# Seven block products in place of eight in 20 of 22 blocks of an FFN's up product, and a down product in three groups

## The chip, the cores and the metric

The kernel runs on one core of a Trainium2 chip. The metric is the device time of one launch in microseconds (us). Before the change three runs took 1074.0, 1075.09 and 1076.6 us; 1075.09 us is the median. The profile is of one further execution on the chip. Engines are named PE (matrix products), PEld (its weight loads), ACT (ScalarE), DVE (VectorE), POOL (GpSimd) and SP (which issues most transfers).

## The reference

One layer of a decoder step for 512 prompt tokens and 8 sequences of 4 new tokens, 544 columns in all. Two mixers (gated linear attention and dilated window attention) come first; the change is in the FFN at the end:

```python
x = x + g1 * (merged @ w_out)
h2 = _rmsnorm(x, norm2_g) * (1 + sc2) + sh2
u1, u2 = jnp.split(h2 @ w_up, 2, axis=-1)
x = x + g2 * ((jax.nn.silu(u1) * u2) @ w_down)
```

With `D_MODEL` 1024 and `D_FF` 2816, `w_up` is 1024 x 5632 and `w_down` 2816 x 1024. A last norm gives the output `y`. Everything is float32.

## The kernel before

Activations lie feature-major: a tile is 128 features by T = 544 columns (NH = 272 is a half). A float32 product is made from three float32r products: each operand is split into a rounded part `hi` and a rest `lo` (ACT casts, DVE subtracts), and PE adds `hi*hi`, `hi*lo` and `lo*hi` in PSUM.

`fm_tile` (L480) makes one 128-row output tile: for every block of 128 inputs six matmuls (`mm_k`, L474, L476, L478), three for each half of the columns. The two halves go to the two banks of one PSUM tile `mm`, of which there are two; a second pool, `sd`, has four one-bank tiles. Weights stream in pieces of 1 MB through three `raw` buffers (L409); `w_split` splits chunks of 128x1024 ahead of their use (ACT L421, DVE L422) into two `hi` and two `lo` buffers.

The order of each engine's work is the order in which the program issues it (`manual_schedule`); waits between engines are put in by the tile layer. In `ffn` (L1694):

- Three up tiles are made by column halves, while the modulated input `h2` is still being finished (L1718 to L1720). Then 41 up tiles follow by `fm_tile`, 8 inputs each, in the order u1, u2 of block 0, of block 1 and so on. `up_evac` takes Silu of u1 (ACT L1688), multiplies by u2 (DVE L1690) and splits the result (ACT L495, DVE L496).
- Seven down tiles follow, 22 inputs each; `residual` (DVE L1546 to L1554) adds them to `x`.
- The last down tile is made half by half (`half_tile`, L1610 to L1612), so that the output of the first half (`out`, L1757) is computed beside the second half's matmuls.

`mid` (L1614) makes the tiles ahead of the FFN; its two last tiles go half by half too (`last_two`, L1596).

Of the kernel before, what the change touches and what calls it, by code (L numbers as in the profile page):

```python
# [6 lines left out]
F32 = mybir.dt.float32  # L7
F32R = mybir.dt.float32r
AF = mybir.ActivationFunctionType
# [4 lines left out]
D = 1024  # L14
NP = 512
# [34 lines left out]

def up_order():
    seq = []
    for m in range(KF):
        seq += [("u1", m), ("u2", m)]
    return seq
# [15 lines left out]
def prep(inp):  # L71
# [32 lines left out]
    wu = inp["w_up"][0]  # L104
    uo = [wu[:, (0 if n == "u1" else DFF) + 128 * m:(0 if n == "u1" else DFF) + 128 * (m + 1)] for n, m in up_order()]
    u3 = slab(np.concatenate(uo[:3], 1))
    sl += wos[:6] + [u3[:, :1024]] + wos[6:] + [u3[:, 1024:]] + [slab(u) for u in uo[3:]]
    wd = inp["w_down"][0]
    sl += [slab(wd[:, 128 * m:128 * (m + 1)]) for m in range(7)]
    wl = np.zeros((128, 24 * 128), f)  # L110
    wl[:, :KF * 128] = slab(wd[:, 896:])
    A["wlast"] = np.ascontiguousarray(wl.reshape(128, 6, 512).transpose(1, 0, 2))
    cols = np.concatenate(sl, 1)
# [204 lines left out]
class Body:  # L318
# [78 lines left out]
    def w_init(self):  # L397
        self.raw = {}
        self.chunks = {}
        self.npiece = 0  # L400
        self.nchunk = 0
        self.pos = 0
        self.total = self.I["wst"].shape[0]

# [8 lines left out]
    def w_split(self, upto):  # L413
        while self.nchunk <= min(upto, 2 * self.total - 1):
            c = self.nchunk
            p = c // 2
            self.w_dma(p + 1)
# [167 lines left out]
    def run(self):  # L585
        nc, tc, I, O = self.nc, self.tc, self.I, self.O
        with ExitStack() as es:
            P = lambda **k: es.enter_context(tc.tile_pool(**k))
            self.cp = P(name="const", bufs=1)
            self.sm = P(name="small", bufs=2)  # L590
            self.heap = P(name="heap", bufs=59)
            self.rawp = P(name="rawp", bufs=3)
            self.hip = P(name="hip", bufs=2)
# [10 lines left out]
            self.heap2 = P(name="heap2", bufs=14)  # L604
            self.ffn()

# [1038 lines left out]
    def h2_half(self, k, half):  # L1645
# [13 lines left out]
        if half == 1:  # L1659
# [7 lines left out]
            nc.gpsimd.tensor_copy(hi[:, NP:T], self.xs[:, k, :])  # L1667
            nc.gpsimd.tensor_sub(lo[:, NP:T], self.xs[:, k, :], hi[:, NP:T])

        def rest():  # L1670
# [9 lines left out]
    def up_evac(self, n, m, halves, hs=(0, 1)):  # L1680
# [10 lines left out]
        if n == "u2" and hs[-1] == 1:  # L1691
            self.act[m] = self.split(self.su.pop(m), "act", self.heap2 if m < 7 else None)

    def ffn(self):  # L1694
# [3 lines left out]
        self.su = {}  # L1698
        uo = up_order()
        ps3 = [[t] for t in self.halves(self.mm()) + [self.mm()[:, 0, :NH]]]  # L1700
        ws = self.ws3
        for half in range(2):
# [3 lines left out]
            if half == 1:  # L1706
                for i in range(3):
                    self.up_evac(*uo[i], ps3[i], (0,))
                    ps3[i].append(self.sd()[:, :NH])
                self.w_split(self.pos // 8 + 1)  # L1710
            c0, c1 = self.COLS[half]
            seq = [(k, m) for k in range(KD) for m in range(3)]
            seq = [(0, 0), (0, 1), (1, 0), (1, 1), (0, 2), (1, 2)] + seq[6:]
            for k, m in seq:
# [6 lines left out]
                if (half, k, m) == (0, 2, 0):  # L1721
                    self.last_rstd(1)
        h2 = self.h2
        self.h2 = self.xa = self.ws3 = None
        self.rst = self.ssq = self.sqh = ws = None
        L0.append(self.copy_rest())
        for i in range(3):
            self.up_evac(*uo[i], ps3[i], (1,))
        for i in range(3, 2 * KF):
            ps = self.fm_tile(h2)  # L1730
            self.up_evac(*uo[i], self.halves(ps))
            self.pump()
        h2 = None
        act = self.act
        ws = []
        L1.append(self.last_weights(ws))
        for m in range(7):
            ps = self.fm_tile(act)
            for h in range(2):
                self.residual(ps[:, h, :NH], self.G2, m, h)  # L1740
            self.sumsq_add(m)
            nc.scalar.mul(self.x[m], self.x[m], self.c("nfg")[:, m:m + 1])
            if m == 6:
                self.act_set(6)
            self.pump()
        while any(self.lanes) or self.late:
            self.pump()

        def out(half):
            c0, c1 = self.COLS[half]  # L1750
            x7 = self.x[7][:, c0:c1]
            nc.scalar.mul(x7, x7, self.c("nfg")[:, 7:8])
            for j in range(4):
# [7 lines left out]

        pss = [self.mm()[:, 0, :NH] for _ in range(2)]
        self.sqh = {}
        for half in range(2):
            ps = pss[half]
# [7 lines left out]
            if half == 0:  # L1773
                self.sqh[7] = self.t2("sq")
            nc.scalar.activation(self.sqh[7][:, c0:c1], self.x[7][:, c0:c1], AF.Square)
        self.last_rstd(1, self.sqh[7])
        out(1)

    def last_weights(self, ws):

        prev = None
        for i in range(7):
            nxt = None
            if i < 6:
# [37 lines left out]
```

## Time and profile before

| what | value |
|---|---|
| median of three runs | 1075.09 us |
| the profiled execution | 1073.69 us |
| its span, first to last instruction | 1071.9 us |
| mean granted PE clock | 0.994 |
| PE busy, matmuls | 1054.3 us (98%), 8505 |
| DVE busy | 447.3 us (42%) |
| ACT busy | 374.9 us (35%) |
| POOL busy | 154.2 us (14%) |

Busy shares are means over stages. A PE matmul row has the time from its start to its modelled end, and matmuls overlap: the distance between starts is the pace. A time such as 652.59 is microseconds from the start of the span. The FFN's plain up tiles run from 679.64 to the end of the up product, the down tiles after them to about 1060.3.

### The profile page before, as it was taken

What the parts mean: (1) busy time and instruction counts of PE and PEld (TensorE: products, weight loads), DVE (VectorE), ACT (ScalarE), POOL (GpSimd) and SP (SyncE); (2) the same over time, 40 slices, a digit from 0 to 9 for tenths busy, and PEclk for the clock granted to TensorE, in tenths of its full rate; (3) what the DMA queues carried; (4) which work ended last, traced back from release to release, by engine and by line L of the source; (5) the groups of instructions that cost most, each with busy time, mean ns of one, the idle gap of its engine ahead of it and who ended that gap; (6) DMA issues with size and microseconds to landing.
All of it is one profiled execution on the core that took longest, in us unless ns stands there. A gap on an engine that the chain in (4) does not pass through costs nothing.

```text
span 1071.9 us, 19534 instructions
## 1 busy us (share of the span) xinstructions
PE 1054.3 (98%) x8505; PEld 988.1 (92%) x8505; DVE 447.3 (42%) x696; ACT 374.9 (35%) x600; POOL 154.2 (14%) x203
## 2 busy tenths in 40 slices
PE   9999999999999999999999999999999999999996
PEld 8788679999989999998989999999999999999995
DVE  5562333444442476353225767433233333332333
ACT  5561214444426432541143335422222323232322
POOL 2302003442332000110011431100000000000101
PEclk9999999999999999899999999999999999999998
DMA  9746563441124427725886563265322222332202
GB/s 375 306 147 237 182 241 127 144 164 65 64 79 162 155 83 239 276 99 150 290 304 207 192 221 153 104 251 235 138 79 106 91 79 79 108 119 90 98 1 84
DMA packets 48701, 169.60 MB, mean 158 GB/s; under 512 B 4124, under 2 KB 27004, under 8 KB 33260
## 3 DMA queue, kind: packets, MB, share of 16 engines
q1 hardware_dynamic: 47928, 167.43, 43.3%
q8 instruction: 67, 1.10, 0.4%
q10 hardware_dynamic: 688, 0.93, 0.3%
q14 instruction: 18, 0.15, 0.0%
HBM read 144.29 MB, written 36.63 MB: 169 GB/s over the span
## 4 chain that ended last, share of the span: by engine, by line
PE 89%; DVE 3%; issue 3%; ACT 2%; POOL 1%; DMA 1%; SPq 0%; DVEq 0%; ACTq 0%; POOLq 0%
PE mm L474 22%; PE mm L478 22%; PE mm L476 22%; PE mm L978 2%; PE mm L980 2%; PE mm L979 2%; PE sd L512 2%; PE sd L1348 1%; POOL o L1390 1%; PE sd L841 1%; PE sd L957 1%; PE sd L825 1%; PE sd L1175 1%; PE sd L1180 1%; POOL sq L1383 1%
## 5 line engine op out<-in xcount | busy, mean ns | idle before, releaser
L422 DVE TENSOR_TENSOR lo<-raw,hi 128x1024 fp32r<-128x1024 f32 x132 | 164.1, 1244 | 191.1 <-ACT hi L421 190.7
L421 ACT CAST hi<-raw 128x1024 fp32r<-128x1024 f32 x132 | 138.3, 1049 | 96.7 <-PE mm L476 91.8
L474 PE MATMUL mm<-hh,hi 128*128 128x272 f32 x656 | 139.2, 293 | 1.3 <-ACT lr L728 1.0
L474 PE MATMUL mm<-h2h,hi 128*128 128x272 f32 x656 | 136.0, 288 | 0.0
L476 PE MATMUL mm<-hl,hi 128*128 128x272 f32 x656 | 135.8, 288 | 0.0
L478 PE MATMUL mm<-hh,lo 128*128 128x272 f32 x656 | 135.7, 288 | 0.1
L476 PE MATMUL mm<-h2l,hi 128*128 128x272 f32 x656 | 135.4, 288 | 0.0
L478 PE MATMUL mm<-h2h,lo 128*128 128x272 f32 x656 | 135.3, 287 | 0.0
L474 PEld LDWEIGHTS mm<-hh,hi 128*128 128x128 f32 x656 | 102.5, 188 | 9.4 <-issue 4.0
L478 PEld LDWEIGHTS mm<-hh,lo 128*128 128x128 f32 x656 | 103.0, 188 | 0.3 <-DVE lo L422 0.3
L476 PEld LDWEIGHTS mm<-h2l,hi 128*128 128x128 f32 x656 | 103.1, 188 | 0.0
L476 PEld LDWEIGHTS mm<-hl,hi 128*128 128x128 f32 x656 | 102.8, 188 | 0.0
L474 PEld LDWEIGHTS mm<-h2h,hi 128*128 128x128 f32 x656 | 102.7, 188 | 0.0
L478 PEld LDWEIGHTS mm<-h2h,lo 128*128 128x128 f32 x656 | 102.7, 188 | 0.0
L1563 POOL TENSOR_TENSOR sq<-sq,sq 128x544 f32<-128x544 f32 x11 | 15.0, 1364 | 365.8 <-ACT sq L1559 365.8
L474 PE MATMUL mm<-acth,hi 128*128 128x272 f32 x308 | 63.8, 288 | 0.0
L476 PE MATMUL mm<-actl,hi 128*128 128x272 f32 x308 | 63.7, 288 | 0.0
L478 PE MATMUL mm<-acth,lo 128*128 128x272 f32 x308 | 63.7, 288 | 0.0
L1051 ACT ACTIVATE qs<-mm,ca 32x544 f32<-32x544 f32 x48 | 33.9, 707 | 56.4 <-PE mm L478 51.2
L495 ACT CAST acth<-su 128x544 fp32r<-128x544 f32 x22 | 14.3, 649 | 110.8 <-DVE su L1690 110.8
L978 PE MATMUL mm<-hi,hh 128*128 128x512 f32 (+1 forms) x128 | 49.0, 383 | 0.0
L478 PEld LDWEIGHTS mm<-acth,lo 128*128 128x128 f32 x308 | 48.3, 188 | 0.0
(354 smaller groups left out, 1832.9 us busy)
## 6 DMA issues: line engine op xcount, KB each, us to landing
raw<-in_wst_dram SPq DMA_DIRECT2D x69, 1024.0 KB, 4.8
ada<-in_wada_dram SPq DMA_DIRECT2D x24, 1024.0 KB, 7.2
out_rest_dram<-in_rest_dram SPq DMA_DIRECT2D x16, 768.0 KB, 7.0
out_kn_dram<-kg SPq DMA_DIRECT2D x5, 1024.0 KB, 6.0
x<-in_xT_dram SPq DMA_DIRECT2D x16, 272.0 KB, 5.2
kg<-in_kg_dram SPq DMA_DIRECT2D x4, 1032.0 KB, 9.4
s<-in_s_dram SPq DMA_DIRECT2D x4, 1024.0 KB, 5.0
vg<-in_vg_dram SPq DMA_DIRECT2D x4, 1024.0 KB, 5.9
```

Source lines behind the costliest of these rows:

```text
L421: self.nc.scalar.copy(hi, src)
L422: self.nc.vector.tensor_sub(lo, src, hi)
L474: nc.tensor.matmul(outs[h], lhsT=wh, rhs=xh[:, h * NH:(h + 1) * NH], start=first, stop=False)
L476: nc.tensor.matmul(outs[h], lhsT=wh, rhs=xl[:, h * NH:(h + 1) * NH], start=False, stop=False)
L478: nc.tensor.matmul(outs[h], lhsT=wl, rhs=xh[:, h * NH:(h + 1) * NH], start=False, stop=last)
L495: self.nc.scalar.copy(hi, src)
L512: nc.tensor.matmul(pa[32 * j:32 * j + 32, :256], lhsT=c[:, 32 * k:32 * k + 32], rhs=w[:, 256 * k:256 * k + 256], start=(k < 4), stop=(k >= 4))
L978: nc.tensor.matmul(out(tt), lhsT=xh, rhs=wh, start=(k == 0), stop=False)
L979: nc.tensor.matmul(out(tt), lhsT=xh, rhs=wl, start=False, stop=False)
L980: nc.tensor.matmul(out(tt), lhsT=xl, rhs=wh, start=False, stop=(k == KD - 1))
L1051: nc.scalar.activation(self.two(qs)[32 * q:32 * q + 32], ps[32 * s:32 * s + 32, :, :NH], AF.Identity, bias=b[32 * s:32 * s + 32])
L1563: nc.gpsimd.tensor_add(self.ssq, self.ssq, s)
```

## The change

For the blocks 2 to 21 the pair of up tiles (u1, u2) is seen as a 2 x 2 product: the inputs in two halves (features 0 to 511 and 512 to 1023), the columns in two halves, and the outputs u1 and u2. Strassen's scheme (in Winograd's form) makes it from seven products of half the input depth, M1 to M7, in place of eight. A product is 4 input blocks x 3 matmuls = 12 matmuls of 272 columns; a block takes 84 matmuls in place of 96. The sums that it needs:

- of inputs, once: `combos` makes eight tiles `ta`, `tb` (POOL L1725, DVE L1726 to L1730) and splits them;
- of weights, per block: `s_sums` (four POOL instructions of 128x512); the seven weight operands are split by `s_a`, `s_b`, `s_c` (128x1024 each) and `s_d` (128x512);
- of outputs, per block: M1+M2, and the sums over M5, M6, M3, M7, M4, which PE accumulates in the two banks `a` and `c` of one `mm` tile, with copies of partial sums by ACT (L1811, L1829, L1832) and sums by DVE (L1824, L1838, L1841).

The down product is made in groups of 8, 8 and 6 blocks, each for all eight output tiles, and added to `x` by `residual`; so the residual step runs 24 times in place of 8. The last group ends with two tiles half by half (`down_last`). `hip` has three buffers in place of two, `heap` 62 in place of 59.

```diff
+GROUPS = [range(0, 8), range(8, 16), range(16, KF)]
...
+    def s_mm(self, n, i, out, first=True, last=True):
+        wh, wl = self.W[n].pop(i)
+        for k in range(4):
+            w = slice(128 * k, 128 * k + 128)
+            xh, xl = self.s_in(i, k)
+            for j, (a, b) in enumerate(((wh, xh), (wh, xl), (wl, xh))):
+                nc.tensor.matmul(out, lhsT=a[:, w], rhs=b, start=first and k == 0 and j == 0,
+                                 stop=last and k == 3 and j == 2, skip_group_check=True)
...
+    def s_first(self, n):
+        ps = self.mm()
+        a = ps[:, 0, :NH]
+        self.s_mm(n, 1, a)
+        t = self.t2("sA")
+        self.nc.scalar.copy(t[:, :NH], a)
+        self.open[n] = (a, ps[:, 1, :NH], t)
+
+    def s_run(self, run, after):
+        nc = self.nc
+        for n, nxt in zip(run, run[1:] + [None]):
+            if nxt:
+                self.s_sums(nxt)
+            a, c, t = self.open.pop(n)
+            su, u, s5 = self.t2("su"), self.t2("u"), self.t2("s5")
+            b = self.sd()[:, :NH]
+            self.s_mm(n, 2, b)
+            nc.vector.tensor_add(su[:, :NH], b, t[:, :NH])
+            nc.scalar.activation(su[:, :NH], su[:, :NH], AF.Silu)
+            if nxt:
+                self.s_a(nxt)
+            self.s_mm(n, 5, c)
+            nc.scalar.copy(s5[:, :NH], c)
+            self.s_d(n)
+            self.s_mm(n, 6, a, False)
+            nc.scalar.copy(t[:, NH:], a)
+            if nxt:
+                self.s_b(nxt)
+            else:
+                after()
+            self.s_mm(n, 3, c, False)
+            nc.vector.tensor_add(su[:, NH:], c, t[:, NH:])
+            nc.scalar.activation(su[:, NH:], su[:, NH:], AF.Silu)
+            self.s_mm(n, 7, a, False)
+            nc.vector.tensor_add(u[:, NH:], a, s5[:, :NH])
+            nc.vector.tensor_mul(u[:, NH:], u[:, NH:], su[:, NH:])
+            if nxt:
+                self.s_c(nxt)
+                self.s_first(nxt)
+            self.s_mm(n, 4, a, False)
+            nc.vector.tensor_mul(u[:, :NH], a, su[:, :NH])
+            self.act[n] = self.split(u, "act")
...
     def ffn(self):
...
+        self.s_sums(2)
+        self.TC = []
+        for q in range(4):
+            self.TC.append(self.combos(q))
+            if q == 1:
+                for i in range(3):
+                    self.up_evac(*UP0[i], ps3[i], (1,))
+        self.s_a(2)
+        ps = self.fm_tile(self.h2)
+        self.up_evac(*UP0[3], self.halves(ps))
+        self.s_b(2)
+        self.s_first(2)
+        self.s_c(2)
...
-        for m in range(7):
+        for m in range(6):
...
-            self.half_tile(ps, act, ws, half, 0, 12)
-            if half == 1:
-                self.last_rstd(0, self.sqh[7])
-                out(0)
-            self.half_tile(ps, act, ws, half, 12, KF)
-            self.residual(ps, self.G2, 7, half)
+            for m in (6, 7):
+                o = ps[m][:, half, :NH]
+                self.half_tile(o, act, ws[n * (m - 6):n * (m - 5)], half)
+                if (half, m) == (1, 6):
+                    self.last_rstd(0, sq[1])
+                    out(0)
+                self.residual(o, self.G2, m, half)
```

On PE, an up tile of before, where rows of all 8 inputs follow each other; `[waits ...]` names the engine whose count an instruction waits for:

```order
L474 MATMUL mm_7817<-h2h_6717,hi_7761 128x272 x2
L476 MATMUL mm_7817<-h2l_6718,hi_7761 128x272 x2
L478 MATMUL mm_7817<-h2h_6717,lo_7762 128x272 x2
L474 MATMUL mm_7817<-h2h_6723,hi_7761 128x272 x2
L476 MATMUL mm_7817<-h2l_6724,hi_7761 128x272 x2
```

And now, in one block: the last matmul of M2 (into an `sd` tile), and the first ones of M5, M6, M3, M7 and M4; between them stand the other 11 of each product, and the next block's M1 ahead of M4:

```order
L1795 MATMUL sd_8844<-h2h_6771,lo_8727 128x272
L1795 MATMUL mm_8802<-tch_7002,hi_8762 128x272 [waits Activation_49]
...
L1795 MATMUL mm_8802<-tch_7002,hi_8762 128x272 [waits Activation_49]
...
L1795 MATMUL mm_8802<-h2h_6753,hi_8796 128x272 [waits Activation_49]
...
L1795 MATMUL mm_8802<-tch_7006,hi_8796 128x272 [waits DVE_49]
...
L1795 MATMUL mm_8802<-tch_7006,wh_8876 128x272 [waits DVE_49]
```

Where an up tile waited for a weight chunk at most, PE now waits for ACT or DVE at the head of five of seven products. M6, M3 and M7 each write to the bank of `mm_8802` other than the one that has just been read.

On ACT, the same stage before, two up tiles and what lies between:

```order
L1688 ACTIVATE su_8752<-mm_8699 128x272 x2
L421 CAST hi_8756<-raw_8526 128x1024
L495 CAST acth_8812<-su_8752 128x544
L421 CAST hi_8817<-raw_8643 128x1024
L1688 ACTIVATE su_8869<-mm_8816 128x272 x2
```

And now one block (`acth` is the split of the block ahead; L1825 and L1839 are the two Silu; the casts of L1760 and L1781 are weight splits):

```order
L1811 COPY sA_8681<-mm_8668 128x272
L516 CAST acth_8696<-u_8573 128x544
L1825 ACTIVATE su_8708<-su_8708 128x272
L1760 CAST hi_8726<-raw_8611 128x1024
L1829 COPY s_1021_8710<-mm_8668 128x272
L1781 CAST wh_8743<-raw_8427 128x512
L1832 COPY sA_8681<-mm_8668 128x272
L1760 CAST hi_8762<-S_8701 128x512
L1760 CAST hi_8762<-S_8702 128x512
L1839 ACTIVATE su_8708<-su_8708 128x272
L1760 CAST hi_8796<-S_8703 128x512
L1760 CAST hi_8796<-raw_8611 128x512
```

Three copies of PSUM halves and 3.5 chunks of weights stand where an up tile pair had two Silu and two chunks; the copy L1829 stands behind a cast of 1024 columns.

On DVE, the place where the modulated input is done, before (L422 splits a weight chunk):

```order
L1671 SCALAR_TENSOR_TENSOR h2l_6768<-h_787_6769,B_130,h2h_6767 128x240
L1690 TENSOR_TENSOR su_6893<-mm_6741,su_6893 128x272
L422 TENSOR_TENSOR lo_6902<-raw_6515,hi_6901 128x1024
L422 TENSOR_TENSOR lo_6906<-raw_6515,hi_6905 128x1024
L1690 TENSOR_TENSOR su_6893<-sd_6897,su_6893 128x272
```

And now (the first of four `combos` and the last row of the part, the split that M1 of block 2 needs; L1728 needs a difference by POOL, which follows four weight sums there):

```order
L1694 SCALAR_TENSOR_TENSOR h2l_6772<-h_787_6773,B_130,h2h_6771 128x240
L1713 TENSOR_TENSOR su_6905<-mm_6745,su_6905 128x272
L443 TENSOR_TENSOR lo_6914<-raw_6515,hi_6913 128x1024
L1726 SCALAR_TENSOR_TENSOR tb_6997<-h_778_6755,dB_6742,h_763_6714 128x272
L1728 SCALAR_TENSOR_TENSOR ta_6996<-h_778_6755,B_130,ta_6996 128x272
L1730 SCALAR_TENSOR_TENSOR tb_6997<-h_778_6755,B_130,ta_6996 128x272
L517 TENSOR_TENSOR tcl_7003<-ta_6996,tch_7002 128x544
L517 TENSOR_TENSOR tcl_7007<-tb_6997,tch_7006 128x544
...
L1761 TENSOR_TENSOR lo_7060<-raw_6591,hi_7059 128x1024
```

Twenty combination and split instructions, and two of an up tile, now stand ahead of the split of the first block's weights.

## Rows read from the trace of the kernel before

**Rows 1.** The page, busy time by engine: us, share of the span, instructions.
```profile
PE 1054.3 (98%) x8505; PEld 988.1 (92%) x8505; DVE 447.3 (42%) x696; ACT 374.9 (35%) x600; POOL 154.2 (14%) x203
```

**Rows 2.** Windows: stretch, length, busy us (count) by engine, clock, DMA share, GB/s.
```profile
750.00:800.00 50.00, 50.00 (x400) 50.00 (x400) 15.86 (x20) 12.91 (x20) 0.00 (x0) 1.00 0.32 117
```

**Rows 3.** Groups, 700 to 1072 us: count, busy us, mean ns, idle before.
```profile
L422 DVE TENSOR_TENSOR lo<-raw,hi 128x1024 fp32r<-128x1024 f32 x58 | 71.1, 1226 | 138.3 <-ACT hi L421 138.3
L421 ACT CAST hi<-raw 128x1024 fp32r<-128x1024 f32 x58 | 60.9, 1050 | 56.4 <-PE mm L476 56.4
L1690 DVE TENSOR_TENSOR su<-mm,su 128x272 f32<-128x272 f32 x38 | 15.0, 437 | 59.7 <-PE mm L478 59.7
L496 DVE TENSOR_TENSOR actl<-su,acth 128x544 fp32r<-128x544 f32 x20 | 14.5, 726 | 14.4 <-ACT acth L495 14.4
L1688 ACT ACTIVATE su<-mm 128x272 f32<-128x272 f32 x38 | 13.1, 395 | 68.4 <-PE mm L478 68.4
L495 ACT CAST acth<-su 128x544 fp32r<-128x544 f32 x19 | 12.3, 649 | 99.3 <-DVE su L1690 99.3
L1790 DVE TENSOR_TENSOR wl<-wlast,wh 128x512 fp32r<-128x512 f32 x6 | 4.3, 709 | 13.8 <-ACT wh L1789 13.8
L1789 ACT CAST wh<-wlast 128x512 fp32r<-128x512 f32 x6 | 3.6, 608 | 0.0
```

**Rows 4.** Timeline at an up tile's end: start, us, engine, instruction.
```profile
727.60 0.41 PE L478 MATMUL mm<-h2h,lo 128*128 128x272 f32 x2
727.85 0.41 PE L474 MATMUL mm<-h2h,hi 128*128 128x272 f32 x2
728.05 0.69 ACT L1688 ACTIVATE su<-mm 128x272 f32<-128x272 f32 x2 [3.60 <-PE mm L478]
728.62 1.05 ACT L421 CAST hi<-raw 128x1024 fp32r<-128x1024 f32 x1
```

**Rows 5.** Timeline, the half-by-half tiles 6 and 7 of the tiles ahead.
```profile
652.04 0.49 DVE L1546 SCALAR_TENSOR_TENSOR x<-mm,G,x 128x272 f32<-128x272 f32 x1
652.05 0.29 PE L1612 MATMUL mm<-mgh,wl 128*128 128x272 f32 x1
...
652.59 0.39 PE L1610 MATMUL mm<-mgh,wh 128*128 128x272 f32 x1 [0.25 <-DVE x L1546]
...
652.82 0.29 PE L1611 MATMUL mm<-mgl,wh 128*128 128x272 f32 x1
```

**Rows 6.** Timeline, a POOL sum beside four DVE subtractions.
```profile
642.36 1.36 POOL L1563 TENSOR_TENSOR sq<-sq,sq 128x544 f32<-128x544 f32 x1 [0.56 <-ACT sq L1559]
...
642.76 3.32 DVE L447 TENSOR_TENSOR wl<-raw,wh 128x512 fp32r<-128x512 f32 x4 [1.24 <-ACT wh L446]
```

**Rows 7.** Timelines of DVE, POOL and PE at the start of the up product.
```profile
674.54 0.47 DVE L1671 SCALAR_TENSOR_TENSOR h2l<-h,B,h2h 128x240 fp32r<-128x240 f32 x1 [0.19 <-ACT h2h L1658]
...
675.35 0.25 POOL L1668 TENSOR_TENSOR h2l<-hs,h2h 128x32 fp32r<-128x32 f32 x1
...
679.64 0.41 PE L474 MATMUL mm<-h2h,hi 128*128 128x272 f32 x2
```

**Rows 8.** Windows with little PE work: at tiny matmuls, after them, and at gaps.
```profile
435.00:437.00 2.00, 2.00 (x13) 2.00 (x13) 0.43 (x1) 0.98 (x1) 0.00 (x0) 1.00 1.04 387
437.00:443.00 6.00, 6.00 (x27) 5.98 (x28) 0.17 (x1) 4.81 (x14) 0.35 (x2) 0.51 0.55 219
...
604.00:608.00 4.00, 3.25 (x24) 3.03 (x24) 2.69 (x4) 1.30 (x2) 3.08 (x2) 1.00 0.92 304
```

**Rows 9.** Timelines of PE, DVE and ACT at the end.
```profile
1055.57 0.62 PE L1598 MATMUL sd<-sq,ones 128*128 128x272 f32 x2
...
1060.14 0.29 PE L1612 MATMUL mm<-acth,wl 128*128 128x272 f32 x1
...
1057.74 3.40 DVE L1757 TENSOR_TENSOR yout<-x,rst 128x272 f32<-128x272 f32 x6 [5.98 <-ACT rst L1602]
1061.07 0.46 DVE L1549 SCALAR_TENSOR_TENSOR x<-mm,G,x 128x240 f32<-128x240 f32 x1
...
1061.88 0.43 ACT L1775 ACTIVATE sq<-x 128x272 f32<-128x272 f32 x1 [3.83 <-DVE x L1554]
```

More of the change, by code (lines that the diff above doesn't have):

```diff
@@ L48, with ffn_order @@
 GB_ORDER += [("pb", m) for m in range(4, 8)]
-def up_order():
+UP0 = [("u1", 0), ("u2", 0), ("u1", 1), ("u2", 1)]
+GROUPS = [range(0, 8), range(8, 16), range(16, KF)]
+def ffn_order():
     seq = []
-    for m in range(KF):
-        seq += [("u1", m), ("u2", m)]
+    f = 2
+    for i, g in enumerate(GROUPS):
+        top = min(g[-1] + 1, KF - 1)
+        while f <= top:
+            seq.append(("S", f))
+            f += 1
+        seq.append(("D", i))
     return seq
@@ new lines, in s_raw, with s_sums @@
+    def s_raw(self, n):
+        p = self.spiece_of[n]
+        self.w_dma(p + 1)
+        return self.raw[p]
+    def s_sums(self, n):
+        nc = self.nc
+        raw = self.s_raw(n)
+        seg = [raw[:, 512 * i:512 * i + 512] for i in range(4)]
+        S = [self.t2("S")[:, :512] for _ in range(3)]
+        nc.gpsimd.tensor_add(S[0], seg[0], seg[3])
+        nc.gpsimd.tensor_sub(S[1], S[0], seg[1])
+        nc.gpsimd.tensor_sub(seg[0], seg[1], seg[0])
+        nc.gpsimd.tensor_sub(S[2], seg[2], S[1])
+        self.S[n] = S
@@ new lines, in s_pair, with s_a @@
+    def s_pair(self, srcs):
+        hi = self.hip.tile([128, 1024], F32R, tag="hi", name="hi_%d" % self.bump())
+        lo = self.hip.tile([128, 1024], F32R, tag="lo", name="lo_%d" % self.bump())
+        c = 0
+        for s in srcs:
+            w = s.shape[-1]
+            self.nc.scalar.copy(hi[:, c:c + w], s)
+            self.nc.vector.tensor_sub(lo[:, c:c + w], s, hi[:, c:c + w])
+            c += w
+        return [(hi[:, :512], lo[:, :512]), (hi[:, 512:], lo[:, 512:])]
+    def s_a(self, n):
+        w = self.W.setdefault(n, {})
+        w[1], w[2] = self.s_pair([self.s_raw(n)[:, 512:1536]])
@@ new lines, in ffn, with after @@
+        self.s_first(2)
+        self.s_c(2)
+        runs = []
+        for kind, i in order:
+            if kind == "S":
+                if not runs or runs[-1][1] is not None:
+                    runs.append([[], None])
+                runs[-1][0].append(i)
+            else:
+                runs[-1][1] = i
+        for j, (run, g) in enumerate(runs):
+            self.pos += 16 * len(run)
+            def after():
+                self.nchunk = self.pos // 8
+                self.w_split(self.nchunk)
+            self.s_run(run, after)
+            if j + 1 < len(runs):
+                self.down(g, runs[j + 1][0][0])
+            else:
+                self.h2 = self.TC = None
+                self.down_last(g)
@@ new lines, in down @@
+    def down(self, g, nxt):
+        act = [self.act[f] for f in GROUPS[g]]
+        for m in range(8):
+            if m == 5:
+                self.s_sums(nxt)
+            elif m == 6:
+                self.s_a(nxt)
+            elif m == 7:
+                self.s_b(nxt)
+            ps = self.fm_tile(act)
+            for h in range(2):
+                self.residual(ps[:, h, :NH], self.G2, m, h)
+            self.pump()
+        for f in GROUPS[g]:
+            self.act[f] = None
+        self.s_first(nxt)
+        self.s_c(nxt)
@@ L1735, in ffn, with down_last @@
+    def down_last(self, g):
+        nc, O = self.nc, self.O
+        act = [self.act[f] for f in GROUPS[g]]
+        self.act = None
+        n = len(act)
+        nfg = self.c("nfg")
+        end = self.pos + 8 * n
         ws = []
-        L1.append(self.last_weights(ws))
-        for m in range(7):
+        for c in range((end - 2 * n) // 8 + 1, end // 8):
+            self.skip.add(c)
+        for m in range(6):
             ps = self.fm_tile(act)
```

158 lines of the change are left out of this document (109 added, 49 removed).

## The prediction, made before the changed kernel ran

> **What bounds the kernel now.** I read the page's busy time first: PE is at work for 98% of the span, DVE and ACT for less than half [rows 1]. Then windows of the up product: 50 us hold 400 matmuls, so one matmul of 272 columns takes a slot of 0.125 us, at the full granted clock, and PE never waits [rows 2]. A matmul's own row is longer (0.29 us) because matmuls overlap; the slot is the price. So in the FFN a removed matmul is worth 0.125 us, and any wait of PE is paid in full, since nothing there is slack. ACT and DVE run at a third of their time, in groups whose durations I use below [rows 3].
>
> What has to be known besides is the price of a hand-over, PE to a reader of PSUM and back, because the new order has many. Out: the last matmul of an up tile starts at about 727.73, the next slot begins at 727.85, and ACT starts to read at 728.05, which is 0.20 us after the slot's end [rows 4]. Back: in the half-by-half tiles ahead of the FFN PE stands until DVE's residual ends at 652.53, starts its matmul at 652.59, and its second one at 652.82 in place of 0.125 us later; so the work resumes as if at 652.695, 0.165 us after the reader's end [rows 5]. The same rows show something that matters more: the residual reads the first half of tile 6 (one bank) and the matmul that waits writes its second half (the other bank). The wait is kept for the whole two-bank tile, not for the bank.
>
> **What goes.** 20 blocks lose 12 matmuls each: 240 x 0.125 = 30.0 us less.
>
> **What comes on PE's path.** In the new block M5 writes bank c; then ACT copies c (L1829); then M6 writes bank a of the same tile. As the tile is guarded as a whole, M6 waits for the copy of c, and the new order shows a wait for ACT just there. In the same way M3 waits for ACT's copy of a after M6 (L1832), and M7 for DVE's sum over c after M3 (L1838). These three hand-overs have nothing of PE's between write and read to hide them. M5 waits for a copy that has all of M2 as cover, and M4 for a sum that has the next block's M1, so these two are free, except in the last block of each of the three runs, where no M1 follows.
>
> Bare, a hand-over costs 0.20 + reader + 0.165: 0.76 us with ACT's 0.395 for 272 columns out of PSUM (three; the copy itself has no row here, and L1688 is the nearest), 0.80 with DVE's 0.437 [rows 3 to 5]. Three of them: 2.32 us a block at the least.
>
> Two of the readers stand in a queue as well. I lay one block out, with 0 at the end of the previous block's M4:
> - M2 fills 0 to 1.50, M5 1.50 to 3.00. DVE multiplies (0.20 to 0.64), ACT casts (to 1.32), DVE splits (1.35 to 2.08): these belong to the previous block and stand ahead. Then DVE's sum for M2 (to 2.44), ACT's Silu (2.47 to 2.87), ACT's cast of 1024 columns for the next block (a following instruction starts 0.12 early, as at 728.62 [rows 4], so 2.78 to 3.83), and only then the copy of c, 3.73 to 4.13. M6 resumes at 4.29: 1.29 us lost.
> - M6 to 5.79, copy 5.99 to 6.38, M3 at 6.55: 0.76 lost.
> - M3 to 8.05. Meanwhile ACT makes two casts of 0.608 and DVE two subtractions of 0.709, which end at about 8.27; the sum over c is ready at 8.25 and ends at 8.7. M7 at 8.85: 0.80 lost, with nothing to spare.
> - M7, the next M1 and M4 follow without a gap to 13.35.
>
> So a block takes 13.35 us in place of 96 x 0.125 = 12.0, with 10.5 of matmuls and 2.85 of waits. A last block of a run lacks two weight splits ahead of the copy but waits for M4's sum, about 3.4 of waits.
>
> To this comes POOL. Its four weight sums a block run beside DVE's subtractions. Four subtractions beside one POOL sum of 1.36 us took 3.32 us, 0.83 each, against 0.709 alone [rows 3, 6], so a sum costs a busy DVE some 0.5 us. DVE is busy for about 8 of 13 us in a block, and only what stands ahead of the two readers counts; I take 0.35 a block, between 0 and 1.0. That makes 3.2 a block, 64 us for 20 blocks; the ends are 2.3 (bare; 46 us) and 3.9 (78 us).
>
> The Trainium skill ("SBUF — State Buffer", section "Who interferes with whom") says that a DVE instruction with two SBUF inputs and a GpSimd instruction that reads SBUF take one shared port in turn, and that whoever comes second is held for the whole instruction. The row of the POOL sum shows a loss of 0.5 us, less than the whole 1.36; by the rule a whole sum would be lost, which is the third rival below.
>
> **The start of the blocks**, once. Before, PE went from the half tiles into plain up tiles at 679.64 [rows 7], needing only weights. Now, after one up tile of 48 slots (6.0 us, so until 685.6), M1 needs weights whose split stands behind all four `combos`. POOL is free at 675.6 [rows 7]; its four sums of 512 columns (1.28 each, from 1.36 for 544 [rows 6]) and one difference of 272 (0.7) end at 681.4. From there DVE has 11 sums of 272 (0.42 each back to back, estimated from 0.437), 8 splits of 0.726, an up tile's product and split (0.44 + 0.73) and the weight split of 1.23: 12.8 us, with some 1.5 us of hand-overs to ACT and back, to 695.7. PE stands for 10 us. After a stretch with only tiny matmuls the clock fell to half, the lower of its two levels (1.2 for 2.4 GHz), and 27 matmuls took 6.0 us, where 0.125 each would make 3.4 [rows 8]: 2.6 us more. I take 12. If POOL holds nobody up, the gap is about 6; with hand-overs twice as long, 16.
>
> **The end.** Before, the output of the first half was computed under 30 matmuls; DVE was through with it at 1061.14, the last matmul's slot ended at 1060.27, and the last square began at 1061.88, 1.6 us after it [rows 9]. Now 18 matmuls are the cover, and behind the first half's output DVE has two residuals and a sum. From the end of tile 6's second half: 2.2 us to the output's first multiply (1055.57 to 1057.74 [rows 9]), 3.4 of multiplies, residual 0.8, square 0.43, sum 0.44, residual 0.8: 8.0 us, while PE ends tile 7 after 0.95 (the column sums) + 2.25 = 3.2. So 4.8 in place of 1.6: 3 us more; 1 to 4.
>
> **What hides.** The further weight splits (1.5 chunks a block, 1.6 us of ACT and 1.8 of DVE) lie beside matmuls except where counted. The 16 more residual rounds (1.3 us of DVE each) lie beside down tiles of 6 us. Weights are the same bytes, at most one 1 MB piece per block. The third `hip` buffer can give back at most what PE waits ahead of the FFN for weights, which the trace does not show; I count 0.
>
> **The sum**, against the profiled execution's 1073.69 us: -30 + 64 + 12 + 3 = +49, so about 1122.7; the median stood 1.4 above that execution, and with the same difference I get 1075.1 + 49 = 1124 us. Ends: -30 + 46 + 6 + 1 = +23, 1098; -30 + 78 + 16 + 4 = +68, 1143.
>
> **Rivals.**
> 1. The hand-overs are covered, and the kernel is faster: PE's waits would find their counts already reached. Then the blocks cost 10.5 and the whole is -30 + 12 + 3 = -15, 1060 us. For it: DVE and ACT are idle more than half of the time, and copies are short. Against it: the copy of c cannot begin before M5's last matmul, and M6 is next in line. It decides at 0.75 us of waits a block (15 us over 20 blocks), which is one bare hand-over; the order has three. 6%.
> 2. The granted clock falls in the blocks, because PE pauses three times in each. Then 84 matmuls take 0.222 each, 8 us more a block: 160 if in all, 80 if in half of the time, about 1200 us. Against it: from 604 to 608 PE paused too (24 matmuls where 32 fit), and the clock stayed at 1.00 [rows 8]. 6%.
> 3. A POOL sum holds DVE for its whole length at one of the two queued readers of every block: 1.28 more than 2.85, 4.1 a block, 83 us; -30 + 83 + 15 = +68, 1143 us. 5%.
> 4. Two hand-overs are bare and the third is hidden: 1.5 a block, 30 us, and the start and end nearly hidden too: 1075 to 1090, 3%.
>
> **How the numbers follow.** The forecast, waits of 2.3 to 3.9 us a block, has 80%. The range 1096 to 1146 holds it and rival 3. From no change this kernel can be told at about 0.2%, 2 us. Faster: rival 1, 6%. Same: part of rival 4, 2%. Slower: all else, 92%.
>
> **What would show it.** In the changed profile PE's idle time should be charged to ACT at L1829 and L1832 and to DVE at L1838, about 20 times each, 1.3 to 1.6, 0.8 and 0.8 to 1.1 us long; a block's first matmuls should stand 13.4 to 13.9 us apart. A gap of some 10 us should stand ahead of the first M1, with the clock at half behind it, and the last square should begin about 5 us after the last matmul of the tiles. If these idle rows are missing or shorter than 0.25 us each, the argument on the shared tile is wrong, and with it the sign.

## The result, and the profile after

The changed kernel takes 1159.76 us (median of 4 runs, 1159.48 to 1161.03) where the kernel before takes 1074.55 (1072.35 to 1076.6): a ratio of 1.080, interval 1.077 to 1.082. The prediction was 1124 us, 1096 to 1146: the side is right, the size is not, and the time lies above the range. The profiled executions differ by 1158.2 - 1071.9 = 86.3 us of span, where the sum of the terms had 49.

The page's busy time answers to [rows 1]:

```profile
PE 1056.2 (91%) x8265; PEld 974.0 (84%) x8265; DVE 580.8 (50%) x921; ACT 438.5 (38%) x755; POOL 273.8 (24%) x286
```

PE has 240 instructions less and is busy for 2 us more, 91% of the span in place of 98%. Both matter: it stands idle, and some of its matmuls take longer. The waits of PE say for whom it stands (line and operation that wait, what is waited for, us in total, times, longest):

```profile
PE mm L1795 <- ACT s L1829: 41.1, 20, 3.3
PE mm L1795 <- ACT hi L1760: 18.5, 1, 18.5
PE mm L1795 <- DVE su L1838: 11.4, 20, 0.8
PE mm L1795 <- ACT sA L1832: 9.5, 20, 0.5
PE sd L1620 <- DVE sq L2016: 3.8, 1, 3.8
...
PE mm L1795 <- DVE u L1841: 1.6, 3, 0.5
```

The three hand-overs stand there, 20 times each, on the lines that the prediction named; L1838 and L1832 have the predicted size (0.57 and 0.48 idle, 0.84 and 0.75 with what a wait costs besides, for 0.80 and 0.76). The start is one wait of 18.45. L1829 is 2.06 us on average, over two kinds of block: M6 waits for L1829 for 2.9 to 3.3 us in ten of the 20 blocks, for 2.15 in one, and for 0.5 to 1.4 in the other nine, where the DVE operations ahead of the copy met no POOL sum. A wait costs PE more than the idle time shown: the last matmul of M5 starts at 772.79, so its slot ends at 772.92, and M6 starts at 776.24 with [3.17]: 3.32 us. The next matmul follows after 0.23 in place of 0.125. That is 0.27 us on top of each row.

The ledger lists by what the spans differ: matmuls -30.0; block waits 63.6 idle + 63 x 0.27 = +80.6; start 18.45 + 0.44 + 2 x 0.27 = +19.4; end 3.8 where before had 1.5, +2.3; and about 120 matmuls that follow each other at 0.226 us instead of 0.125, +12.1. Together +84.4 of the 86.3.

One block shows where L1829's 3.17 us come from. The timeline of DVE, ACT and POOL from its POOL sums to M6:

```profile
767.37 1.29 POOL L1749 TENSOR_TENSOR S<-S,raw 128x512 f32<-128x512 f32 x1
767.67 1.30 DVE L1842 TENSOR_TENSOR u<-u,su 128x272 f32<-128x272 f32 x1
768.62 1.50 POOL L1750 TENSOR_TENSOR raw<-raw 128x512 f32<-128x512 f32 x1
...
768.89 1.78 DVE L1761 TENSOR_TENSOR lo<-S,hi 128x512 fp32r<-128x512 f32 x1
770.09 1.73 POOL L1751 TENSOR_TENSOR S<-raw,S 128x512 f32<-128x512 f32 x1
770.60 1.77 DVE L1761 TENSOR_TENSOR lo<-raw,hi 128x512 fp32r<-128x512 f32 x1
772.29 0.43 DVE L1847 TENSOR_TENSOR u<-mm,su 128x272 f32<-128x272 f32 x1
772.75 0.65 ACT L516 CAST acth<-u 128x544 fp32r<-128x544 f32 x1 [3.74 <-DVE u L1847]
773.43 0.72 DVE L517 TENSOR_TENSOR actl<-u,acth 128x544 fp32r<-128x544 f32 x1 [0.71 <-ACT acth L516]
774.08 0.43 DVE L1824 TENSOR_TENSOR su<-sd,sA 128x272 f32<-128x272 f32 x1
774.54 0.43 ACT L1825 ACTIVATE su<-su 128x272 f32<-128x272 f32 x1 [1.14 <-DVE su L1824]
774.88 1.03 ACT L1760 CAST hi<-raw 128x1024 fp32r<-128x1024 f32 x1
775.81 0.38 ACT L1829 COPY s<-mm 128x272 f32<-128x272 f32 x1
776.24 0.39 PE L1795 MATMUL mm<-tch,hi 128*128 128x272 f32 x1 [3.17 <-ACT s L1829]
```

Read it from below: M6 waits for the copy, the copy for the cast of 1024 columns ahead of it on ACT, that for the Silu, this for DVE's sum, and DVE is late because a multiply took 1.30 us and two subtractions 1.78 and 1.77 while POOL made its sums. Each of the three begins beside a POOL sum and ends 0.3 to 0.6 us after that sum has ended (at 768.66, 770.12 and 771.82). It is the queue that the prediction laid out, with every step where it was expected except for those three. In the group view of the blocks (mean ns behind the comma), the changed kernel has:

```profile
L1761 DVE TENSOR_TENSOR lo<-S,hi 128x512 fp32r<-128x512 f32 x60 | 51.6, 888 | 29.8 <-ACT hi L1760 29.8
L1761 DVE TENSOR_TENSOR lo<-raw,hi 128x512 fp32r<-128x512 f32 x20 | 24.6, 1231 | 0.0
L1842 DVE TENSOR_TENSOR u<-u,su 128x272 f32<-128x272 f32 x20 | 17.9, 893 | 2.1
L1841 DVE TENSOR_TENSOR u<-mm,s 128x272 f32<-128x272 f32 x20 | 8.8, 442 | 37.3 <-PE mm L1795 37.3
```

L1842 has two inputs in SBUF and doubles; L1841, just ahead of it, has one in PSUM and keeps its length. The Trainium skill ("SBUF — State Buffer", section "Who interferes with whom") says that "a DVE instruction with two SBUF inputs contends with a GpSimd instruction that reads SBUF"; the trace agrees, 893 against 442 ns.

The clock, in windows behind the same wait one block earlier, where M6 starts at 759.50 after 3.07 us (the last numbers are clock, DMA share, GB/s):

```profile
759.00:760.00 1.00, 0.50 (x4) 0.50 (x5) 0.80 (x1) 0.97 (x3) 0.00 (x0) 1.00 0.00 0
...
761.00:763.00 2.00, 1.53 (x7) 1.21 (x7) 0.26 (x2) 1.18 (x3) 0.00 (x0) 0.50 0.45 86
763.00:764.00 1.00, 1.00 (x7) 1.00 (x6) 1.00 (x2) 0.25 (x1) 0.00 (x0) 0.53 0.96 401
```

M6 begins at 2.4 GHz (granted clock 1.00), and its last matmuls and M3's first run at 1.2 GHz (0.50). In nine of the ten blocks with a wait of 2.9 us or more some matmuls run so, about ten in most and 19 in one; in the tenth (M6 at 898.74, after 3.20 us) the clock stays at 1.00.

The start, which answers to [rows 7]: POOL, DVE and PE.

```profile
681.33 3.37 POOL L1725 TENSOR_TENSOR ta<-h 128x272 f32<-128x272 f32 x4
684.66 1.74 POOL L1748 TENSOR_TENSOR S<-raw 128x512 f32<-128x512 f32 x1
...
695.75 1.82 POOL L1751 TENSOR_TENSOR S<-raw,S 128x512 f32<-128x512 f32 x1
```
```profile
686.91 1.49 DVE L1726 SCALAR_TENSOR_TENSOR tb<-h,dB,h 128x272 f32<-128x272 f32 x1
...
700.27 0.50 DVE L1726 SCALAR_TENSOR_TENSOR tb<-h,dB,h 128x272 f32<-128x272 f32 x1
```
```profile
703.40 0.59 PE L1795 MATMUL mm<-h2h,hi 128*128 128x272 f32 x1 [18.45 <-ACT hi L1760]
704.66 0.59 PE L1795 MATMUL mm<-h2h,lo 128*128 128x272 f32 x1 [0.44 <-DVE lo L1761]
```

After the four differences POOL goes straight on with the sums of the next two blocks, from 684.66 to 697.6, whose weights are already there. Beside them each operation of the combos takes up to three times what it takes once POOL is done (1.49 for 0.50).

### The profile page after: what moved, and what is told of

It reads as the page before. It is cut to its first block, busy times and chain, and to the rows that moved or that the text cites. A ratio compares the mean times of both kernels' runs of the same rounds, so it can differ in the third digit from the quotient of the medians.

```text
span 1158.2 us, 19585 instructions
## 1 busy us (share of the span) xinstructions
PE 1056.2 (91%) x8265; PEld 974.0 (84%) x8265; DVE 580.8 (50%) x921; ACT 438.5 (38%) x755; POOL 273.8 (24%) x286
## 4 chain that ended last, share of the span: by engine, by line
PE 75%; DVE 13%; ACT 6%; issue 4%; POOL 1%; DMA 0%; DVEq 0%; POOLq 0%; ACTq 0%
PE mm L495 14%; PE mm L497 13%; PE mm L499 13%; PE mm L1795 11%; DVE lo L1761 4%; PE mm L1000 2%; ACT hi L1760 2%; PE mm L1001 2%; PE mm L1002 2%; PE sd L533 1%; DVE u L1842 1%; ACT acth L516 1%; PE sd L1370 1%; PE sd L979 1%; DVE su L1838 1%
## 5 line engine op out<-in xcount | busy, mean ns | idle before, releaser
L443 DVE TENSOR_TENSOR lo<-raw,hi 128x1024 fp32r<-128x1024 f32 x92 | 115.1, 1251 | 61.8 <-ACT hi L442 61.1
L1795 PE MATMUL mm<-tch,hi 128*128 128x272 f32 x240 | 76.0, 317 | 52.5 <-ACT s L1829 41.1
L442 ACT CAST hi<-raw 128x1024 fp32r<-128x1024 f32 x92 | 95.7, 1047 | 45.9 <-PE mm L497 45.4
L1795 PEld LDWEIGHTS mm<-tch,hi 128*128 128x128 f32 x240 | 47.5, 198 | 61.3 <-ACT s L1829 45.5
L1795 PE MATMUL mm<-h2h,hi 128*128 128x272 f32 x160 | 51.9, 324 | 28.0 <-ACT hi L1760 18.5
L1795 PE MATMUL mm<-tch,lo 128*128 128x272 f32 x240 | 72.4, 302 | 0.0
L1795 PE MATMUL mm<-tcl,hi 128*128 128x272 f32 x240 | 72.2, 301 | 0.0
L1761 DVE TENSOR_TENSOR lo<-S,hi 128x512 fp32r<-128x512 f32 x60 | 51.6, 888 | 29.8 <-ACT hi L1760 29.8
L1795 PEld LDWEIGHTS mm<-h2h,hi 128*128 128x128 f32 x160 | 33.3, 208 | 33.5 <-ACT hi L1760 18.7
L1761 DVE TENSOR_TENSOR lo<-raw,hi 128x1024 fp32r<-128x1024 f32 (+1 forms) x40 | 49.1, 1228 | 24.5 <-ACT hi L1760 24.3
```

Of the source, the lines that this page charges most:

```text
L1761: self.nc.vector.tensor_sub(lo[:, c:c + w], s, hi[:, c:c + w])
L1795: nc.tensor.matmul(out, lhsT=a[:, w], rhs=b, start=first and k == 0 and j == 0, stop=last and k == 3 and j == 2, skip_group_check=True)
```

## The experiments

Theory A: the whole tile is guarded, so three hand-overs per block are bare. Theory B: POOL's sums lengthen DVE, in the queue ahead of the readers and at the start. Whether the half clock comes of the long pauses is read from the same runs too. C and D are stated where they are tested.

**c in a tile of its own.**

```
-        self.open[n] = (a, ps[:, 1, :NH], t)
+        self.open[n] = (a, self.sd()[:, :NH], t)
```

> The changed kernel with one edit: the accumulators a and c of a block lie in two tiles (c in a one-bank tile of its own) in place of two banks of one. Theory A (PE's three waits a block come from the guard on the whole two-bank tile): M6 and M7 no longer wait; the copy of c (L1829) is then waited for by M3, with all of M6 as cover. Of some 3.9 us of waits a block about 1 to 2 stay, where POOL's weight sums delay DVE and with it the copy. Time about 1095 us, 1080 to 1115. Rival (the waits are ACT's and DVE's queues being late, whatever the tile): M3 waits for the copy nearly as long as M6 does now, and the time stays above 1140 us.

Measured: 1081.45 us (1080.43 to 1082.18), 1.006 of before (1.004 to 1.007): 78.3 us less by one line. The waits of PE (largest first):

```profile
PE mm L1795 <- ACT hi L1760: 18.5, 1, 18.5
PE mm L1795 <- DVE u L1841: 7.7, 11, 1.3
...
PE sd L1795 <- ACT s L1829: 1.2, 2, 0.6
```

Of 63.6 us of block waits 8.9 are left, 13 in number, and the clock of the blocks is 1.00, with POOL as busy in this window as in the changed kernel (23.53 us; its row stands at the next experiment):

```profile
880.00:960.00 80.00, 78.03 (x618) 77.36 (x617) 45.19 (x74) 30.28 (x53) 23.53 (x15) 1.00 0.29 101
```

So A holds: without the shared tile the same queue of ACT and DVE, beside the same POOL sums, costs 8.9 us of waits in the blocks.

**POOL's weight sums left out**, the tile still shared.

```
-        S = [self.t2("S")[:, :512] for _ in range(3)]
-        nc.gpsimd.tensor_add(S[0], seg[0], seg[3])
-        ...
-        self.S[n] = S
+        self.S[n] = [seg[0], seg[3], seg[2]]
```

> The changed kernel without POOL's four weight sums a block (raw weight segments stand in for the sums; the up product of these blocks is therefore another one; PE, ACT and DVE have the same work). Theory B (POOL's sums hold DVE's subtractions of two SBUF operands for about the length of a POOL instruction): DVE's 512-column subtractions go from 0.89 to about 0.70 us in the mean, the wait at L1829 from 2.06 to about 1.0 us, the gap ahead of the first M1 from 18.5 to about 9 us, and the granted clock stays at full in the blocks. Time about 1120 us, 1105 to 1135. Rival (the sums are not what delays DVE; the queue order alone does): above 1150 us.

Measured: 1114.62 us (1113.1 to 1116.0), 1.036 (1.035 to 1.038). The weight operands are raw segments here, so the result of these blocks is another one; the work of PE, ACT and DVE is the same. The waits, the groups of DVE that answer to those above, and M6 of two blocks in a row:

```profile
PE mm L1790 <- ACT s L1824: 18.8, 20, 1.4
PE mm L1790 <- DVE su L1833: 11.4, 20, 0.8
PE mm L1790 <- ACT sA L1827: 9.5, 20, 0.5
PE mm L1790 <- ACT hi L1755: 7.6, 1, 7.6
```
```profile
L1756 DVE TENSOR_TENSOR lo<-raw,hi 128x512 fp32r<-128x512 f32 x80 | 51.6, 687 | 23.6 <-ACT hi L1755 23.6
L1837 DVE TENSOR_TENSOR u<-u,su 128x272 f32<-128x272 f32 x20 | 8.9, 443 | 2.1
L1836 DVE TENSOR_TENSOR u<-mm,s 128x272 f32<-128x272 f32 x20 | 8.8, 442 | 37.2 <-PE mm L1790 37.2
```
```profile
700.67 0.39 PE L1790 MATMUL mm<-tch,hi 128*128 128x272 f32 x1 [0.72 <-ACT s L1824]
...
714.01 0.40 PE L1790 MATMUL mm<-tch,hi 128*128 128x272 f32 x1 [1.00 <-ACT s L1824]
```

The block is 714.01 - 700.67 = 13.34 us long; the prediction's layout without POOL had 13.35. Waits with their 0.27 come to 41.3 + 17.0 = 58.3 us, 2.9 a block for a predicted 2.85. So POOL's sums cost, of the 45 us: 22.3 in the blocks' waits, 10.9 at the start and about 10 in the clock; some 2 are not accounted for. With pauses of 1.4 us at most no matmul of the blocks runs at half clock, but for some 16 behind the start's wait of 7.6; the window of the blocks 880 to 960 has 1.00, the changed kernel's (the second row) 0.91:

```profile
880.00:960.00 80.00, 69.70 (x523) 66.24 (x523) 39.90 (x68) 33.08 (x60) 0.00 (x0) 1.00 0.23 80
```
```profile
880.00:960.00 80.00, 60.38 (x412) 56.90 (x413) 47.35 (x60) 31.00 (x60) 23.26 (x16) 0.91 0.19 66
```

B holds. The half clock in the blocks goes with the long pauses, which either edit takes away, and not with POOL's work, which the first edit leaves in place.

**Both edits together.**

> Both edits: two tiles and no weight sums. If A and B are all there is beside the removed matmuls, PE goes through a block in 10.5 us with little waiting, and what is left is the gap ahead of the first M1 (about 9 us, and some 2.6 us at half clock behind it) and the end (3 us): 1074.5 - 30 + 15 = about 1060 us, 1052 to 1075. If something else holds PE in the blocks (weights, matmul pace in one bank), it stays above 1080 us.

Measured: 1058.79 us (1058.5 to 1058.83), 0.985 (0.983 to 0.986). Of the 30 us of matmuls 16.6 arrive; what is missing is the start (7.6 idle and some 17 matmuls at half clock behind it), the end and 1.6 us of small waits. A block starts 10.53 us after the last one, where its 84 slots make 10.5. The two edits overlap: alone they gave 78.3 and 45.1 us, together 101.0. Without the shared tile POOL's sums cost 1081.45 - 1058.79 = 22.7 us, half as much as with it.

**The down product in groups alone**, with all up tiles plain.

```
             if kind == "S":
 ...
+                for u in ("u1", "u2"):
+                    ps = self.fm_tile(self.h2)
+                    self.up_evac(u, i, self.halves(ps))
+                    self.pump()
 ...
-            self.s_run(run, after)
```

> Only the second part of the change: the up product by plain tiles as before, the down product in groups of 8, 8 and 6 blocks with the new end. Theory: the 16 more residual rounds lie beside down tiles, so only the end costs, about 3 us: 1077.5 us, 1074 to 1081. Rival (the groups cost at each of their 24 tiles, by a wait for PSUM or for weight chunks): over 1085 us.

Measured: 1080.99 us (1080.36 to 1082.39), 1.005 (1.004 to 1.007), 5.6 us above before in that comparison (1075.35). The wait for the last square is 3.8 us in place of 1.5, near the 3 more that I gave it; 3.0 us more come from a place that I had not counted, the second up tile behind the half tiles (at 687.70), whose weight split is issued late (2.5 for ACT, 0.5 for DVE; some 12 matmuls at half clock behind them).

**The start alone**, on top of the two tiles.

```
-        self.s_sums(2)
 ...
+        self.TC.append(self.combos(0))
+        self.up_evac(*UP0[3], self.halves(ps))
+        self.TC.append(self.combos(1))
+        ps = self.fm_tile(self.h2)
+        self.TC.append(self.combos(2))
+        self.up_evac("u1", 2, self.halves(ps))
+        self.TC.append(self.combos(3))
 ...
+        self.s_sums(3)
+        self.s_a(3)
         ps = self.fm_tile(self.h2)
 ...
+        self.up_evac("u2", 2, self.halves(ps))
```

> Base: the changed kernel with c in a tile of its own (1081.45 us). On top only the start of the blocks: block 2 is computed plainly (12 matmuls more, 1.5 us), its two tiles stand between the combos as cover, the combos' differences on POOL stand ahead of the weight sums, and the combos spread over three tiles. Theory C (most of what that kernel still loses is the 18.5 us gap ahead of the first M1 and the half clock behind it): the gap row is gone or below 2 us, and the time falls by 18.5 + 0.5 + some 5 us of half clock - 1.5, to about 1059 us (1054 to 1065). Theory D (POOL's sums beside DVE's subtractions in the blocks carry the remaining loss, the start is only where it shows first): the waits move into the blocks, and the time stays above 1070.

Measured: 1070.88 us (1068.61 to 1072.54), 0.997 (0.996 to 0.998). Neither theory held as it was written: the 18.45 us are gone, but two other waits stand in their place, 5.09 for a weight split of block 2 behind the combos and 2.22 for one of block 3. POOL's sums only moved: they run from 679.15 to 693.26 now, and the combos beside them are as long as before (1.5 to 1.8 us).

**Two of the four weight sums on DVE**, in `s_c`, on top of the two tiles.

```
-        nc.gpsimd.tensor_sub(seg[0], seg[1], seg[0])
-        nc.gpsimd.tensor_sub(S[2], seg[2], S[1])
 ...
+        nc.vector.tensor_sub(S[2], raw[:, 1024:1536], S[1])
+        nc.vector.tensor_sub(raw[:, :512], raw[:, 512:1024], raw[:, :512])
```

> Base: the changed kernel with c in a tile of its own (1081.45 us). On top only this: two of the four weight sums of a block (the two that the last split needs) go from POOL to DVE, 2 x 0.69 us a block, and POOL keeps two. Theory: POOL and DVE lengthen each other, so work that DVE takes over at 0.69 us costs DVE less than the lengthening that it ends (0.69 became 1.3 to 1.8 us beside a POOL sum). The 7.7 us of waits for DVE's L1841 in the blocks go to below 2, the gap at the start falls from 18.5 to 10 to 14 as half of POOL's work there goes, sum about 1070 us (1064 to 1076). Rival: DVE, with 1.4 us more a block, becomes the one that PE waits for in the blocks; then 1082 or above, with waits for DVE in nearly all of the blocks.

Measured: 1068.8 us (1068.69 to 1068.94), 0.995 (0.994 to 0.997), 12.7 less than with all on POOL (about 11 by the ratios to the kernel before, which ran 1.4 us faster here than beside the two tiles). The waits for L1841 went from 7.7 to 1.6 us, the start from 18.5 to 13.0. 1.4 us more work a block on DVE costs less than the lengthening that it ends.

**All four on DVE** (these two in `s_b`), on the second kernel of "All together" below, which takes 1062.36 us with two on DVE.

```
-        nc.gpsimd.tensor_add(S[0], seg[0], seg[3])
-        nc.gpsimd.tensor_sub(S[1], S[0], seg[1])
 ...
+        nc.vector.tensor_add(S[0], raw[:, :512], raw[:, 1536:])
+        nc.vector.tensor_sub(S[1], S[0], raw[:, 512:1024])
```

> Base: the kernel of the run before this one, with all four weight sums of a block on DVE, none on POOL: 4 x 0.69 = 2.8 us of DVE a block, and no POOL beside it. If it is the sharing between POOL and DVE that costs, this is no slower than with two on POOL: DVE has some 6.1 + 2.8 = 8.9 us of work in a block of 10.5. About 1056 us (1052 to 1062). If DVE's load decides, PE waits for DVE in most blocks and it is above 1065.

Measured: 1074.51 us (1073.84 to 1075.53), 1.000 (0.999 to 1.001). The rival wins: DVE is now what the blocks wait for, through ACT's copy behind it:

```profile
PE sd L1798 <- ACT s L1832: 13.0, 13, 3.4
```

Of the three splits tried, two on POOL is the best: it beats four on the kernel with two tiles, and none on the second kernel with everything together.

**The end, first try**, on the kernel with groups alone: pair 2 of the first half's output goes behind tile 6, pair 3 behind tile 7.

```
-                    out(0)
+                    out(0, (0, 1))
                 self.residual(o, self.G2, m, half)
                 ...
+                if half == 1:
+                    out(0, (m - 4,))
```

> Base: the kernel with plain up tiles and the down product in groups of 8, 8 and 6 (1080.99 us), that is without Strassen. On top only the order at the end: of the first half's output, the multiplies of the third pair stand behind the residual of tile 6 and those of the fourth behind that of tile 7, where all stood ahead of both. If the 3.8 us that PE waits there for the last square is DVE's queue, as the prediction has it, the wait falls to about 2 and the time by 1.5 to 2.5 us, to 1078.5 to 1079.5. If it is the chain residual, square, sum itself, nothing changes.

Measured: 1081.47 us (1080.29 to 1081.67) beside 1080.99: nothing. The wait fell from 3.8 to 2.8 us, but the last output's multiplies began at 1072.48 after 1072.20: three multiplies (2.31 us beside POOL's two) still stood ahead of tile 6's residual, and two behind the last one.

**The end, second try**: the whole output of the first half behind tile 7's residual.

```
-                    out(0)
 ...
+        out(0)
         self.last_rstd(1, sq[1])
         out(1)
```

> Base: plain up tiles with the down product in three groups (1080.99 us). Only the end: the whole output of the first half stands behind the residual of tile 7 and ahead of the last column sum. The wait for the last square (3.8 us) falls to about 1.5 and the time by 2 to 3 us, to 1078 to 1079. If the multiplies do not fit beside the last chain (square, column sum, two ACT steps), they delay the last output by what they overhang, and nothing is gained: 1081, as in the first try at the end.

Measured: 1077.05 us (1074.96 to 1078.38), 1.002 (1.0015 to 1.003), 3.9 less, a little more than expected. Its rows of DVE and PE answer to [rows 9]:

```profile
1065.94 0.47 DVE L1571 SCALAR_TENSOR_TENSOR x<-mm,G,x 128x240 f32<-128x240 f32 x1 [0.15 <-PE mm L1634]
...
1066.65 2.19 DVE L1969 TENSOR_TENSOR yout<-x,rst 128x272 f32<-128x272 f32 x6
1067.24 0.72 PE L1622 MATMUL sd<-sq,ones 128*128 128x272 f32 x2 [0.68 <-ACT sq L1984]
...
1068.99 3.33 DVE L1969 TENSOR_TENSOR yout<-x,rst 128x272 f32<-128x272 f32 x6
```

The six multiplies lie in the 2.2 us in which the square, the column sum and ACT's two steps run, and the last output begins at 1068.99 in place of 1072.20.

**All together**: two tiles, two sums on DVE, block 2 plain, and the end by the first try; then the end by the second try, with block 3's weight sums and the weight splits earlier at the start:

```
         self.up_evac(*UP0[3], self.halves(ps))
+        self.w_split(self.pos // 8 + 1)
         self.TC.append(self.combos(1))
         ...
+        self.s_sums(3)
         ...
+        self.s_a(3)
         self.TC.append(self.combos(3))
         ps = self.fm_tile(self.h2)
+        self.s_b(3)
         self.up_evac("u2", 2, self.halves(ps))
```

> All together, with the whole result computed: c in a tile of its own, two of four weight sums on DVE, block 2 plain with the combos spread beside it, and the end in the other order. 19 Strassen blocks save 19 x 1.5 = 28.5 us of matmuls. If the hand-overs, POOL's sums beside DVE, the start and the end are all that the change lost, what is left is some 3 us of end and some 2 of small waits: 1075 - 28.5 + 5 = about 1051 us (1046 to 1058), faster than both kernels. If something else was lost besides, above 1060.

> Base: the version with all four mends (1064.09 us). Two orders differ. At the start the next weight split stands ahead of the combos of the second chunk, and the first split of block 3 ahead of the last combos: its three waits of 2.0, 1.5 and 2.0 us there, with some 3 us of half clock behind them, should go to below 1.5 us in sum. At the end the whole output of the first half stands behind the residual of tile 7, where the engines wait for the last column sum: the wait for the last square falls from 2.8 us to below 1.5, and as the multiplies fit beside that chain, the last output begins 2 us earlier. Together 5 to 9 us less, about 1057 us (1053 to 1061). If POOL's sums lengthen whatever DVE does at the start, so that the order matters little, 1062 or above.

Measured: 1064.09 us (1062.64 to 1069.39), 0.992 (0.989 to 0.995), and 1062.36 (1061.99 to 1066.04), 0.989 (0.987 to 0.991). Both are faster than the kernel before, by about 1%, and both miss what was expected, by 6 and by 1.4 us above the range; both times lie where the other case of the expectation was put (above 1060, and 1062 or above). In the second, PE is busy for 99% of the stretch 720 to 1040 (first a window, then PE's waits):

```profile
720.00:1040.00 320.00, 315.89 (x2482) 312.02 (x2482) 196.88 (x357) 136.00 (x246) 55.93 (x36) 1.00 0.34 123
```
```profile
PE sd L1798 <- ACT s L1832: 5.6, 2, 3.6
PE mm L1798 <- DVE lo L1761: 2.1, 1, 2.1
```

19 blocks save 28.5 us, and 11 of them arrive in its span. Most of the rest lies in the first two blocks: 8.4 us of waits for splits and copies behind the combos (5.6 and 2.1 above, and 0.7), and some 30 matmuls at half clock after them (3.1). Later blocks start 10.83 us apart where 10.53 was seen without sums: M3 reaches its copy just as it ends, shows next to no idle time and still loses 0.3 us (at 737.31 the starts are 0.33 and then 0.23 apart in place of 0.125), some 4 us in all. Moving the first sums and splits forward only moved the waits (8.0 us in the first of the two kernels) to other instructions; how much of them could be hidden stays open.

## Why the prediction was wrong

- **The matmuls that go**, -30.0: right. PE has 240 instructions less, and without the shared tile and the sums a block takes 10.53 us.
- **Three hand-overs per block at one tile**: right, to the place, the number and the bare price; the one-line edit takes away 68.2 of the 80.6 us of block waits (8.9 + 13 x 0.27 are left). The layout without POOL gave 13.35 us a block, measured 13.34.
- **"I take 0.35 a block, between 0 and 1.0"**, POOL's sums: this step failed. They cost 22.3 / 20 = 1.1 us a block in waits, above the upper bound. I took the price from [rows 6], one POOL sum beside four DVE subtractions, and spread it over the block. That row was read wrongly already. The first of its four subtractions, asked for by itself, is the row that stands below this list: it took 1.51 us, and the other three share the remaining 1.9 us, 0.6 each. That is about 0.8 more than the 0.709 alone, and the sum, begun at 642.36, had 0.96 us left to run. So the loss was not 0.5 spread over four but nearly all of what was left of the sum, on one instruction. In the changed kernel the sums run back to back, and in the long blocks three DVE operations in one chain ahead of the copy at L1829 meet them: 1.30 for 0.44, 1.78 and 1.77 for 0.69. The rule of the Trainium skill that stands above was weighed against that row, and it was the better guide. Rival 3 had its mechanism and gave it one sum per block, at 5%. That its 4.1 us of waits a block came near the measured 80.6 / 20 = 4.0 is in part luck: the mean is made of ten long blocks, which lose more than one sum's length, and others that lose little or none.
- **The start, 12**: 21.3 (19.4 and some 19 matmuls at half clock). The same error in another place: "POOL is free at 675.6 ... end at 681.4" counted the first block's sums only. POOL went straight on with the sums of two more blocks, and without any sum the gap is 7.6, near the 6 that I gave for POOL holding up nobody.
- **The clock in the blocks**, 0 in the sum: about 10 us. Rival 2 rested on the pauses; I held [rows 8] against it, where short pauses left 1.00, and gave it 6%. They leave 1.00 here too, up to 2.15 us; behind the 3 us pauses, which exist only with POOL's lengthening, the clock fell nine times of ten. The rival was right in kind and its 80 us far too large.
- **The end, 3**: 2.3 in the wait; right, within the 1 to 4. The late weight split in the groups' kernel is a wait of its own (3.0) that I did not list; in the changed kernel the 18.45 us cover that place.
- **Forecast of the rows**: L1829 at 1.3 to 1.6 was 2.06 as a mean, and near 1.0 or near 3.1 in most single blocks; block starts at 13.4 to 13.9 apart were 776.24 - 759.50 = 16.7 in a contended block (from M6 to M6).

The row of the first subtraction in [rows 6]:

```profile
642.76 1.51 DVE L447 TENSOR_TENSOR wl<-raw,wh 128x512 fp32r<-128x512 f32 x1 [1.24 <-ACT wh L446]
```

The three misses add up: 16.6 in the waits, 9.3 at the start, 10 in the clock, less 0.7 at the end, are 35 of the 37 us between +49 and +86.

## What to carry to other kernels

When a change makes one engine read what another has just written, ask what the unit of the guard is: two banks in one tile made three bare hand-overs a block out of an order that hides them in two tiles. Before reading a price out of a merged row (x4 here), ask for its instructions one by one: a mean can hide one long wait. Before work goes to an engine that is idle, list which instructions of the busy one will run beside it and at what length, along the chain that ends at the wait, not as an average over the block. And an engine that is given work for later blocks does it as soon as its order and its data allow; here that put the cost of two blocks' sums beside the combos at the start.

## What was not expected of the hardware

DVE operations on two SBUF inputs take up to 1.5 us beside POOL sums in place of 0.50 (272 columns), and up to 1.78 in place of 0.69 (512 columns); POOL's own go from 1.28 to as much as 1.82. So both slow down, and an operation with one PSUM input stays at 0.44. In the changed kernel nine of ten pauses of PE of 2.9 to 3.3 us were followed by matmuls at 1.2 GHz, in most blocks after first ones at 2.4; the tenth (3.20) was not, nor was one of 2.15, nor the pauses up to 1.4. In the kernel with groups alone one of 2.50 was (clock 0.50 from 689 to 691). The length of a pause alone did not decide it here. At the end of the kernel with the second try, six multiplies of two SBUF inputs take 2.19 us with POOL idle and 3.33 beside POOL's two.
